# Stick-breaking weights as running sums against differences of neighbouring values, and adaLN's rows moved to other places in the filler

## The chip, the cores and the metric

One Trainium2 chip, one core. The metric is the device time of one execution in microseconds (us); before: median 1586.23 us of 3 runs (1585.62 to 1587.53). A core has a TensorE (PE) for matrix products, whose weight loads are listed apart as PEld, VectorE (DVE), ScalarE (ACT) and GpSimd (POOL) for elementwise work, and SyncE (SP), which here issues all DMAs. Each runs its instructions in program order; they meet by semaphores.

## The reference, cut to what matters

One layer: adaLN modulation, a projection to queries, keys and values, two attention groups side by side, an output projection, a feed-forward layer. 1024 prompt rows, and 64 sample rows with 1024 cached keys; everything in float32. The change touches the second attention group, "stick-breaking", 8 heads of 64:

```python
z = jnp.einsum('bqhd,bkhd->bhqk', qs.astype(f32), ks.astype(f32)) * scale
earlier = k_pos[None, :] < q_pos[:, None]
log_keep = jnp.where(earlier, jax.nn.log_sigmoid(-z), 0.0)
between = lax.cumsum(log_keep, axis=3, reverse=True) - log_keep
w = jnp.where(earlier, jnp.exp(jax.nn.log_sigmoid(z) + between), 0.0)
osb = jnp.einsum('bhqk,bkhd->bqhd', w, vs.astype(f32))
```

With s = sigmoid(z) and k = sigmoid(-z) = 1 - s: the weight of key j is s[j] times the product of k over all later keys that the query may see. The other place is adaLN, `silu(c) @ w_ada + b_ada`: six vectors of 1024 for each of two requests, from a weight of 1024 x 6144.

## The kernel before

The program has three stages: the attention (to some 720 us), the output projection with the second normalisation (to some 840 us), and the feed-forward layer (to the end).

The attention goes through eight units: units 0 to 3 are the four differential heads, units 4 to 7 are pairs of stick-breaking heads. A unit has eight steps for the prompt and one for the samples, put somewhere into the next unit's steps (those of units 3 and 7 stand near the end of their own). A step of class `Stick` is (u, q, hd): 256 queries, that is two blocks t = 2q and 2q+1 of 128, of one head. Its `score` makes, for each t and each chunk of up to 512 keys, two matmuls (L575, L576) into a PSUM bank, on ACT sigmoid(z) and sigmoid(-z) (L738, L739), on POOL the causal mask of the last 128 columns of both (`earlier`, L720), and then `stick`: on DVE a running product over k from the right (a scan, L712), a multiplication of s by it, shifted by one column (L713), and on POOL one column where two chunks meet (L715). `apply` transposes these weights on PE (L586), splits them into a high and a low part on ACT and DVE (L64, L65; the kernel computes float32 products as sums of products of such parts), and multiplies with the values (L759, L760).

The loop over the steps issues `apply` of one step merged with `score` of the next, and between their pieces a filler: the projections of the coming unit, `proj(u, g)` for three groups g of 384, 384 and 320 rows, each needed at a fixed step (`need`: group 0 at the unit's first step, group 1 at its third, group 2 at its seventh). Each piece is given a cost, and the ratio of the costs to the next need sets how much filler goes beside a step. adaLN's remaining twelve pieces of 256 columns (`ada_rows`, 16 matmuls each from two loads of 512 KB, L197 and L201) are filler too: two behind group 2 of units 2 to 5, one behind that of unit 6, three behind that of unit 7, the last with a due time "end". Values come out of `proj_v` transposed: ACT copies them from PSUM (`vf`, L530), `natural` transposes them on PE (L459, bank `pn`) for the output in memory, and the same bank is split into V's two parts.

What the code issues is then put in order for each engine by the compiler's own model of time, so that the order on an engine follows neither the code's order nor the chip's measured times.

Of the kernel before, what the change touches and what calls it, by code (L numbers as in the profile page):

```python
# [10 lines left out]
F32 = mybir.dt.float32  # L11
# [3 lines left out]
ALU = mybir.AluOpType  # L15

P = 128
D = 1024
KT = D // P
TP = 1024  # L20
# [10 lines left out]
def fr(ap):  # L31
    return ap.bitcast(F32)


def build(tc, I, O):
    nc = tc.nc
    ctx = ExitStack()
    sb = ctx.enter_context(tc.tile_pool(name="sb", bufs=1))
# [8 lines left out]
    def big(name, tag, shape, dt=F32R):  # L47
        return sb.tile(shape, dt, tag=tag, name=name, bufs=BUFS[tag])

    def small(shape, name, tag, dt=F32, bufs=2):  # L50
        return sb.tile(shape, dt, tag=tag, name=name, bufs=bufs)

    def brief(shape, name, tag, dt=F32, bufs=2):
        return atp.tile(shape, dt, tag=tag, name=name, bufs=bufs)

    def bank(name, tag):
        return pp.tile([P, 512], F32, tag=tag, name=name)
# [4 lines left out]
    def split(src, hi, lo, eh=None, el=None):  # L62

        (eh or nc.scalar.copy)(hi, src)  # L64
        (el or nc.vector).tensor_tensor(lo, src, fr(hi), ALU.subtract)  # L65

    def halves(name, n=2):
        return [big(f"{name}_{i}", "s", [P, 512], F32) for i in range(n)]


    ident = sb.tile([P, P], F32, name="ident")
# [24 lines left out]
    def x_rows(m):  # L96
        return (x_p[m * P : (m + 1) * P, :], P) if m < 8 else (x_s, TS)
# [200 lines left out]
    def dense_T(ps, w, act, g, ks=range(KT)):  # L298

        n = GRP[g][1]  # L300
        (wh, wl), (hh, hl) = w, act[g]
        for k in ks:
            mm(ps[:, :n], lhsT=wh[:, k, :], rhs=hh[:, k, :n], start=(k == 0), stop=False)  # L303
            mm(ps[:, :n], lhsT=wh[:, k, :], rhs=hl[:, k, :n], start=False, stop=False)  # L304
            mm(ps[:, :n], lhsT=wl[:, k, :], rhs=hh[:, k, :n], start=False, stop=(k == 7))  # L305
            yield 3 * n / 2400
# [133 lines left out]
    def pad_queries(u, m, t):  # L440
        r = slice(64 * m, 64 * m + 64)
        nc.gpsimd.tensor_copy(QZ[m][r], fr(U[u]["Q"][m][r, P * t : P * t + 2 * P]))  # L442

    def family(u):
        return (0, u * P) if u < 4 else (1, (u - 4) * P)
# [6 lines left out]
    def natural(f, u, g, out, name):  # L452

        fam, uc = family(u)
        c0, n = GRP[g]
        nt = 3 if g < 2 else 2
        pt = bank("pn" + name, "pv")
        for i in range(nt):
            nc.tensor.transpose(pt[:, i * P : (i + 1) * P], f[:, i * P : (i + 1) * P], ident)  # L459
        if g == 2:  # L460
            nc.tensor.transpose(pt[:TS, 256:384], f[:, 256:320], ident)
        o = brief([P, 3, P], "o" + name, "vf", bufs=1)
        ptv = pt[:, :384].rearrange("p (t c) -> p t c", t=3)
        nc.vector.tensor_copy(o[:, :nt], ptv[:, :nt])
        load(out[fam][c0 : c0 + nt * P, uc : uc + P].rearrange("(t p) c -> p t c", p=P), o[:, :nt])
        if g == 2:
            nc.vector.tensor_copy(o[:TS, 2], ptv[:TS, 2])
            load(out[2 + fam][:, uc : uc + P], o[:TS, 2])
        return ptv, o

    U = [dict() for _ in range(8)]

    def proj_q(u, g, wq):
        c0, n = GRP[g]
        qs = -0.125 if u < 4 else 0.125
        if g == 0:
            U[u]["Q"] = [big(f"Q{u}{m}", "qk", [P, TP]) for m in range(2)]
        Q = U[u]["Q"]
        if u + g:
            ps = bank(f"pq{u}{g}", "pj")  # L480
            yield from dense_T(ps, wq, hT, g)
        else:
            ps = PS[0]
        w = min(n, TP - c0)
        for m in range(2):
            r, o = slice(64 * m, 64 * m + 64), slice(64 - 64 * m, 128 - 64 * m)
            nc.scalar.mul(Q[m][r, c0 : c0 + w], ps[r, :w], qs)
            nc.vector.scalar_tensor_tensor(Q[m][o, c0 : c0 + w], ps[r, :w], qs, fr(Q[m][r, c0 : c0 + w]), ALU.mult, ALU.subtract)
        if g == 2:
            qsm = brief([P, TS], f"qsm{u}", "ms", bufs=1)  # L490
            nc.scalar.mul(qsm, ps[:, 256:320], qs)
            load(smD[u, :, 0, :], qsm)

    def proj_k(u, g, wk):
        c0, n = GRP[g]
        if g == 0:
            U[u]["Kd"] = [big(f"K{u}{m}", "qk", [P, TP]) for m in range(2)]
            U[u]["Kl"] = big(f"Kl{u}", "qk", [P, TP])
        Kd, Kl = U[u]["Kd"], U[u]["Kl"]
        if u + g:  # L500
# [18 lines left out]
    def proj_v(u, g, wv):  # L519
        c0, n = GRP[g]  # L520
        if g == 0:
            U[u]["V"] = big(f"V{u}", "v", [P, 8, 2, P])
        V = U[u]["V"]
        if u + g:
            ps = bank(f"pv{u}{g}", "pj")
            yield from dense_T(ps, wv, hT, g)
        else:
            ps = PS[2]
        vf = small([P, 384], f"vf{u}{g}", "kf", bufs=2)
        nc.scalar.copy(vf[:, :n], ps[:, :n])  # L530
        ptv, o = natural(vf, u, g, vout, f"v{u}{g}")
        if g == 2:
            load(smV[u], o[:TS, 2])
        ms = slice(3 * g, min(3 * g + 3, 8))
        src = ptv[:, : ms.stop - ms.start]
        if u < 4:
            h_, l_ = V[:, ms, 0, :], V[:, ms, 1, :]
        else:
            q4 = V.rearrange("p m a (b d) -> p m (a b) d", b=2)
            h_, l_ = q4[:, ms, 0::3, :], q4[:, ms, 1:3, :]  # L540
            src = src.rearrange("p t (a d) -> p t a d", a=2)
        split(src, h_, l_)
        yield 0.33
# [35 lines left out]
    def chunks(W):  # L579
        return [(c, min(512, W - c)) for c in range(0, W, 512)]  # L580
# [124 lines left out]
    def stick(s, kp):  # L705


        n = len(s)
        for c in reversed(range(n)):
            w = s[c].shape[-1]  # L710
            k = kp[c][:, (1 if c == 0 else 0) : w][:, ::-1]
            nc.vector.tensor_tensor_scan(k, k, k, 1.0 if c == n - 1 else kp[c + 1][:, 0:1], ALU.mult, ALU.bypass)  # L712
            nc.vector.tensor_tensor(s[c][:, : w - 1], s[c][:, : w - 1], kp[c][:, 1:w], ALU.mult)  # L713
            if c < n - 1:
                nc.gpsimd.tensor_tensor(s[c][:, w - 1 : w], s[c][:, w - 1 : w], kp[c + 1][:, 0:1], ALU.mult)  # L715

    def earlier(s, kp, n):

        for a, f in ((s, 0.0), (kp, 1.0)):
            nc.gpsimd.affine_select(a, a, pattern=[[-1, n]], compare_op=ALU.is_gt, fill=f, base=0, channel_multiplier=1)  # L720

    class Stick:
# [7 lines left out]
        def score(self):  # L730
            u, q, hd = self.u, self.q, self.hd
            self.w = []
            for t in (2 * q, 2 * q + 1):
                ch = chunks(P * (t + 1))
                s, kp = ([a[:, :w] for a, (_, w) in zip(halves(f"{x}{self.name}{t}", len(ch)), ch)] for x in "sk")
                for c, (c0, w) in enumerate(ch):
                    ps = qk(u, hd, t, c0, w, f"pz{self.name}{t}{c}")
                    nc.scalar.activation(s[c], ps, AF.Sigmoid)  # L738
                    nc.scalar.activation(kp[c], ps, AF.Sigmoid, scale=-1.0)  # L739
                    yield 0.43 * w / 512  # L740
                earlier(s[-1][:, -P:], kp[-1][:, -P:], P)
                stick(s, kp)
                self.w.append(s)

        def apply(self):
# [212 lines left out]
    fill = Filler()  # L958
# [10 lines left out]
    steps = [st for sec in sections for st in sec]  # L969
    need = []  # L970
    for u in range(8):
        sec = [st for st in sections[u] if not isinstance(st, Sample)]
        for st, g in zip((sec[0], sec[2], sec[6]), range(3)):
            need.append((steps.index(st), (u, g)))
    need.append((len(steps) + 1, "end"))
    cost = [st.cost for st in steps]
    drain(proj(0, 0))
    ready_1()
# [2 lines left out]
    rows = chain(gate_rows(2 * D, I["g_post_mix"], "r1", 0, ("s", "s")), mod2)  # L981
    rows2 = gate_rows(5 * D, I["g_post_ffn"], "r2", 1, ("s", "s"))

    def some(rows, n):

        for c in rows:
            if c is None:
                n -= 1
                if n == 0:
                    return  # L990
            else:
                yield c

    others = {2: (rows, 2, 2), 3: (rows, 2, 2), 4: (rows, 2, 2), 5: (rows, 2, 2), 6: (rows, 1, 1), 7: (rows, 3, 3)}
    for u in range(8):
        for g in range(3):
            if u + g:
                fill.add(proj(u, g), 12, (u, g))
            if g == (2) and u in others:
                gen, n, c = others[u]  # L1000
                fill.add(some(gen, n), c, "end" if u == 7 else None)
    steps[0].ready()
    drain(steps[0].score())
    prev = None
# [42 lines left out]
    for m in range(NTT):  # L1047
        g, off = m // 3, (m % 3) * P
        hi, lo = mT[g]
        src, rows = x_rows(m)  # L1050
# [219 lines left out]
```

## Time and profile before

| what | value |
|---|---|
| median of 3 runs | 1586.23 us |
| profiled execution, its span | 1589.58 us, 1587.9 us |
| instructions | 23684 |
| busy PE, PEld, DVE, ACT, POOL | 96%, 86%, 62%, 44%, 23% of the span |
| mean granted TensorE clock | 0.973 |

The median and the profiled execution differ by 3.3 us; 1.7 us of the profiled time lie outside its span. The busy shares are means over three stages that differ: the feed-forward layer, over half of the time, has PE full and DVE half idle, the stick-breaking units have DVE nearly full. A share by stage is therefore read, not that of the whole. [...]

### The profile page before, as it was taken

What the parts mean: (1) busy time and instruction counts of PE and PEld (TensorE: products, weight loads), DVE (VectorE), ACT (ScalarE), POOL (GpSimd) and SP (SyncE); (2) the same over time, 40 slices, a digit from 0 to 9 for tenths busy, and PEclk for the clock granted to TensorE, in tenths of its full rate; (3) what the DMA queues carried; (4) which work ended last, traced back from release to release, by engine and by line L of the source; (5) the groups of instructions that cost most, each with busy time, mean ns of one, the idle gap of its engine ahead of it and who ended that gap; (6) DMA issues with size and microseconds to landing.
All of it is one profiled execution on the core that took longest, in us unless ns stands there. A gap on an engine that the chain in (4) does not pass through costs nothing.

```text
span 1587.9 us, 23684 instructions
## 1 busy us (share of the span) xinstructions
PE 1517.0 (96%) x8682; PEld 1357.9 (86%) x8682; DVE 987.2 (62%) x1880; ACT 703.3 (44%) x1665; POOL 366.7 (23%) x580
## 2 busy tenths in 40 slices
PE   6899999999999999789999999999999999999998
PEld 3689988988888889667889888999999899999896
DVE  3777676778789888995552455445544445544447
ACT  3867675766666667656563221121221121221132
POOL 0444352526353434451120000000000000000003
PEclk9999999998999999879999999999999999999999
DMA  9322142432322222364220222021111011111025
GB/s 309 115 60 87 55 116 84 135 95 76 95 74 85 69 70 78 103 208 161 97 63 27 80 80 78 17 79 53 54 42 52 28 41 53 54 41 53 27 80 179
DMA packets 152518, 133.22 MB, mean 84 GB/s; under 512 B 11233, under 2 KB 136274, under 8 KB 152402
## 3 DMA queue, kind: packets, MB, share of 16 engines
q1 hardware_dynamic: 152402, 131.71, 27.2%
q8 instruction: 68, 1.11, 0.3%
q14 instruction: 48, 0.39, 0.1%
HBM read 108.59 MB, written 23.09 MB: 83 GB/s over the span
## 4 chain that ended last, share of the span: by engine, by line
PE 74%; DVE 12%; issue 4%; ACT 3%; DMA 2%; POOL 1%; SPq 0%; POOLq 0%; DVEq 0%; ACTq 0%
PE pu L303 8%; PE pu L304 8%; PE pu L305 8%; PE pd L1145 8%; PE pd L1146 8%; PE pd L1148 7%; DVE k L712 4%; PE py L1059 2%; PE py L1060 2%; PE pt L586 2%; DVE s L713 2%; PE py L1062 2%; PE pq L304 1%; PE pq L303 1%; PE pq L305 1%
## 5 line engine op out<-in xcount | busy, mean ns | idle before, releaser
L1152 DVE TENSOR_TENSOR acc<-pd,acc 128x512 f32<-128x512 f32 x252 | 171.9, 687 | 113.3 <-PE pd L1148 107.2
L1130 ACT ACTIVATE sq<-pu 128x384 f32<-128x384 f32 (+1 forms) x96 | 45.2, 471 | 310.8 <-PE pu L305 310.8
L1131 DVE TENSOR_TENSOR sq<-sq 128x384 f32<-128x384 f32 (+1 forms) x96 | 72.1, 751 | 174.7 <-ACT sq L1130 174.7
L65 DVE TENSOR_TENSOR al<-pt,ah 128x512 fp32r<-128x512 f32 (+2 forms) x128 | 75.5, 599 | 25.7 <-ACT ah L64 24.9
L575 PE MATMUL pz<-K,Q 128*128 128x512 f32 (+2 forms) x192 | 74.8, 393 | 6.4 <-ACT k L739 2.2
L64 ACT CAST ah<-pt 128x512 fp32r<-128x512 f32 (+2 forms) x128 | 65.4, 523 | 33.6 <-PE pt L586 23.2
L586 PE MATMUL pt<-ident,s 128*128 128x128 f32 x432 | 73.7, 288 | 3.3 <-DVE s L713 2.6
L624 ACT ACTIVATE s<-s,mn 128x512 f32<-128x512 f32 (+3 forms) x96 | 58.5, 611 | 26.7 <-DVE mn L660 25.4
L576 PE MATMUL pz<-Kl,qz 128*128 128x512 f32 (+2 forms) x192 | 69.8, 369 | 0.0
L712 DVE TENSOR_TENSOR_SCAN k<-k 128x127 f32<-128x127 f32 (+3 forms) x64 | 62.1, 980 | 4.3 <-POOL k L720 4.0
L713 DVE TENSOR_TENSOR s<-s,k 128x383 f32<-128x383 f32 (+3 forms) x96 | 62.9, 662 | 1.4
L586 PEld LDWEIGHTS pt<-ident,s 128*128 128x128 f32 x432 | 53.1, 147 | 7.6 <-DVE s L713 3.3
L65 DVE TENSOR_TENSOR rl<-sq,rh 128x384 fp32r<-128x384 f32 x64 | 35.7, 558 | 37.9 <-ACT rh L64 37.9
L738 ACT ACTIVATE s<-pz 128x512 f32<-128x512 f32 (+2 forms) x96 | 48.1, 501 | 16.5 <-PE pz L576 12.0
L575 PEld LDWEIGHTS pz<-K,Q 128*128 128x128 f32 x192 | 38.3, 200 | 15.1 <-ACT k L739 4.5
L64 ACT CAST rh<-sq 128x384 fp32r<-128x384 f32 x64 | 32.9, 514 | 40.2 <-DVE sq L1131 38.2
L739 ACT ACTIVATE k<-pz 128x512 f32<-128x512 f32 (+2 forms) x96 | 48.4, 504 | 4.9 <-DVE k L712 4.0
L442 POOL CAST qz<-Q 64x256 fp32r<-64x256 f32 x64 | 34.7, 542 | 66.3 <-PE pz L576 63.9
L760 PE MATMUL po<-al,V 128*128 128x256 f32 (+1 forms) x160 | 43.5, 306 | 6.7 <-DVE al L65 6.6
L759 PE MATMUL po<-ah,V 128*128 128x256 f32 (+1 forms) x160 | 44.9, 292 | 0.5 <-ACT ah L64 0.5
L720 POOL TENSOR_SCALAR_AFFINE_SELECT s<-s 128x128 f32<-128x128 f32 x64 | 30.1, 470 | 63.6 <-ACT s L738 62.9
L660 DVE CUSTOM_DVE_ANT_0 s<-pz,T 128x512 f32<-128x512 f32 (+3 forms) x64 | 37.2, 585 | 10.8 <-PE pz L576 10.3
(1227 smaller groups left out, 5211.3 us busy)
## 6 DMA issues: line engine op xcount, KB each, us to landing
arr<-in_w_ada SPq DMA_DIRECT2D x16, 512.0 KB
arm<-in_w_ada SPq DMA_DIRECT2D x16, 512.0 KB
ar<-in_w_ada SPq DMA_DIRECT2D x10, 512.0 KB
mixD<-mx SPq DMA_DIRECT2D x32, 128.0 KB
xr<-in_x_prompt SPq DMA_DIRECT2D x16, 256.0 KB
xD<-xr SPq DMA_DIRECT2D x16, 256.0 KB
xy<-xD SPq DMA_DIRECT2D x8, 512.0 KB
out_y_prompt<-xy SPq DMA_DIRECT2D x16, 256.0 KB
```

What stands on the lines that cost most here:

```text
L64: (eh or nc.scalar.copy)(hi, src)
L65: (el or nc.vector).tensor_tensor(lo, src, fr(hi), ALU.subtract)
L303: mm(ps[:, :n], lhsT=wh[:, k, :], rhs=hh[:, k, :n], start=(k == 0), stop=False)
L304: mm(ps[:, :n], lhsT=wh[:, k, :], rhs=hl[:, k, :n], start=False, stop=False)
L305: mm(ps[:, :n], lhsT=wl[:, k, :], rhs=hh[:, k, :n], start=False, stop=(k == 7))
L575: mm(ps[:, :w], lhsT=S["Q"][m][:, qt], rhs=S["Kd"][m][:, c0 : c0 + w], start=True, stop=False)
L586: nc.tensor.transpose(pt[:kr, i * P : (i + 1) * P], a, ident)
L712: nc.vector.tensor_tensor_scan(k, k, k, 1.0 if c == n - 1 else kp[c + 1][:, 0:1], ALU.mult, ALU.bypass)
L1145: mm(ps, lhsT=rh[:, off : off + P], rhs=wh[:, cols], start=(j == 0), stop=False)
L1146: mm(ps, lhsT=rh[:, off : off + P], rhs=wl[:, cols], start=False, stop=(m == 8 and end))
L1148: mm(ps, lhsT=rl[:, off : off + P], rhs=wh[:, cols], start=False, stop=end)
L1152: nc.vector.tensor_tensor(acc[m][:, cols], ps, acc[m][:, cols], ALU.add)
```

## The change

`stick` is replaced, for the prompt, by `taken`. Let C[j] be the sum of the weights of key j and all later ones. Then C[j] = s[j] + k[j] C[j+1], which is one scan with multiply and add; and the sum over j of w[j] v[j] equals the sum over j of C[j] (v[j] - v[j-1]), with v[-1] = 0. So the values are replaced by the differences of neighbouring rows, which POOL makes from `vf` for units 4 to 7 (`df`) and PE transposes into a bank of its own (`pdv`); the bank of `natural` then only serves the output. Only s is masked, since a zero in s keeps the sum at zero wherever the query sees nothing. The samples keep the old form. adaLN's pieces stand one behind group 0 and one behind group 1 of units 2 to 7, and have no due time of their own.

```diff
+    vlast = sb.tile([P, 1], F32, name="vlast")
...
         nc.scalar.copy(vf[:, :n], ps[:, :n])
+        w = min(n, TP - c0)
+        if u >= 4:
+            df = small([P, 384], f"df{u}{g}", "kf", bufs=2)
+            if g == 0:
+                nc.gpsimd.tensor_copy(df[:, 0:1], vf[:, 0:1])
+            else:
+                nc.gpsimd.tensor_tensor(df[:, 0:1], vf[:, 0:1], vlast, ALU.subtract)
+            nc.gpsimd.tensor_tensor(df[:, 1:w], vf[:, 1:w], vf[:, 0 : w - 1], ALU.subtract)
+            if g < 2:
+                nc.gpsimd.tensor_copy(vlast, vf[:, w - 1 : w])
         ptv, o = natural(vf, u, g, vout, f"v{u}{g}")
...
+        if u >= 4:
+            yield 0.33
+            pt = bank(f"pdv{u}{g}", "pj")
+            for i in range(ms.stop - ms.start):
+                nc.tensor.transpose(pt[:, i * P : (i + 1) * P], df[:, i * P : (i + 1) * P], ident)
+            ptv = pt[:, :384].rearrange("p (t c) -> p t c", t=3)
...
+    def taken(s, kp):
+        n = len(s)
+        for c in reversed(range(n)):
+            k, d = kp[c][:, ::-1], s[c][:, ::-1]
+            nc.vector.tensor_tensor_scan(d, k, d, 0.0 if c == n - 1 else s[c + 1][:, 0:1], ALU.mult, ALU.add)
...
-                earlier(s[-1][:, -P:], kp[-1][:, -P:], P)
-                stick(s, kp)
+                d = s[-1][:, -P:]
+                nc.gpsimd.affine_select(d, d, pattern=[[-1, P]], compare_op=ALU.is_gt, fill=0.0, base=0, channel_multiplier=1)
+                taken(s, kp)
...
-    need.append((len(steps) + 1, "end"))
...
-    others = {2: (rows, 2, 2), 3: (rows, 2, 2), 4: (rows, 2, 2), 5: (rows, 2, 2), 6: (rows, 1, 1), 7: (rows, 3, 3)}
     for u in range(8):
         for g in range(3):
             if u + g:
                 fill.add(proj(u, g), 12, (u, g))
-            if g == (2) and u in others:
-                gen, n, c = others[u]
-                fill.add(some(gen, n), c, "end" if u == 7 else None)
+            if u > 1 and g < 2:
+                fill.add(some(rows, 1), 1)
```

First place: VectorE in the last unit, scoring its step q = 3 of the first head. Names read unit, underscore, q, head, t, and then the chunk: s7_306_1 is chunk 1 of block 6. Before:

```order
L712 SCALAR_TENSOR_TENSOR k7_306_1_8809<-k7_306_1_8809 128x384
L65 TENSOR_TENSOR al7_202_8752<-pt7_202_8747,ah7_202_8751 128x384
L713 TENSOR_TENSOR s7_306_1_8807<-s7_306_1_8807,k7_306_1_8809 128x383
L712 SCALAR_TENSOR_TENSOR k7_306_0_8808<-k7_306_0_8808,k7_306_1_8809 128x511
L65 TENSOR_TENSOR al7_210_8803<-pt7_210_8797,ah7_210_8802 128x512
L713 TENSOR_TENSOR s7_306_0_8806<-s7_306_0_8806,k7_306_0_8808 128x511
```

And the same scans now:

```order
L743 SCALAR_TENSOR_TENSOR s7_306_1_8632<-k7_306_1_8634,s7_306_1_8632 128x384
L65 TENSOR_TENSOR al7_202_8597<-pt7_202_8592,ah7_202_8596 128x384
L743 SCALAR_TENSOR_TENSOR s7_306_0_8631<-k7_306_0_8633,s7_306_1_8632,s7_306_0_8631 128x512
L65 TENSOR_TENSOR Vn7_8752<-vn7_8714,Vn7_8752 64x128
L743 SCALAR_TENSOR_TENSOR s7_307_1_8662<-k7_307_1_8664,s7_307_1_8662 128x512
```

The multiplications L713 are gone between the scans; a scan reads k and s, and goes on from the chunk behind it.

Second place: TensorE where one of adaLN's pieces stands (`ar`, `arm`: the loaded weights; `poS`, `pt`: the samples' products and the transposes of a step). Before, behind group 2 of unit 4:

```order
L586 MATMUL pt5_010_6229<-ident_66,s5_010_0_6107 128x128
L586 MATMUL pt5_010_6229<-ident_66,s5_011_0_6140 128x128 x2
L201 MATMUL pam210_6454<-arm2100_6455,sc_106 32x256 x4
L201 MATMUL pam210_6454<-arm2101_6483,sc_106 32x256 x4
L575 MATMUL pz5_2041_6429<-K50_5569,Q50_5448 128x128
```

Now, behind group 1 of unit 4:

```order
L620 MATMUL poS3_4946<-cv30_4842,ahS30_4952 128x256
L459 MATMUL pnv41_5026<-ident_66,vf41_5020 128x128 x3
L551 MATMUL pdv41_5033<-ident_66,df41_5022 128x128 x3
L201 MATMUL pam201_5039<-arm2010_5040,sc_106 32x256 x4
L201 MATMUL pam201_5039<-arm2011_5048,sc_106 32x256 x4
L621 MATMUL poS3_4946<-cv30_4842,alS30_4953 128x128
```

The new transposes of `df` stand right behind those of `vf` in TensorE's queue, and adaLN's piece behind them.

Third place: GpSimd, where the new operations stand among the masks. Before, in unit 7's second q:

```order
L720 AFFINE_SELECT s7_102_0_8399<-s7_102_0_8399 128x128
L715 TENSOR_TENSOR ss6_1_8306<-ss6_1_8306,skt6_8310 128x1
L720 AFFINE_SELECT k7_102_0_8400<-k7_102_0_8400 128x128
L715 TENSOR_TENSOR ss6_0_8305<-ss6_0_8305,sk6_1_8309 128x1
L442 CAST qz0_493<-Q70_7604 64x256
```

Now, in unit 6's last q, with the first group of unit 7's values:

```order
L770 AFFINE_SELECT s6_307_1_7688<-s6_307_1_7688 128x128
L537 COPY df70_7801<-vf70_7799 128x1
L540 TENSOR_TENSOR df70_7801<-vf70_7799 128x383
L542 COPY vlast_499<-vf70_7799 128x1
L770 AFFINE_SELECT s6_316_1_7768<-s6_316_1_7768 128x128
```

Each block has one mask instead of two, and three operations per group of values stand among them.

## Rows read from the trace of the kernel before

**Rows 1.** The page: busy time by engine; tenths in 40 slices; granted clock.
```profile
PE 1517.0 (96%) x8682; PEld 1357.9 (86%) x8682; DVE 987.2 (62%) x1880; ACT 703.3 (44%) x1665; POOL 366.7 (23%) x580
PE   6899999999999999789999999999999999999998
DVE  3777676778789888995552455445544445544447
PEclk9999999998999999879999999999999999999999
```
**Rows 2.** Busy time by stretch; first line: the columns.
```profile
core 0: us, PE busy (x) PEld busy (x) DVE busy (x) ACT busy (x) POOL busy (x), PEclk, DMA share, GB/s
380.00:400.00 20.00, 16.26 (x88) 13.54 (x87) 17.13 (x25) 11.52 (x29) 13.73 (x19) 0.74 0.21 66
400.00:460.00 60.00, 59.24 (x412) 56.00 (x405) 48.16 (x87) 38.80 (x93) 18.96 (x38) 1.00 0.30 90
460.00:490.00 30.00, 24.86 (x169) 21.39 (x168) 29.05 (x45) 19.51 (x48) 18.61 (x25) 0.89 0.49 142
490.00:520.00 30.00, 30.00 (x201) 29.45 (x200) 27.72 (x47) 18.66 (x43) 8.23 (x18) 1.00 0.09 28
520.00:570.00 50.00, 44.09 (x279) 40.81 (x278) 44.78 (x70) 30.54 (x74) 24.12 (x39) 0.90 0.33 97
570.00:630.00 60.00, 59.66 (x407) 58.20 (x406) 51.89 (x89) 42.30 (x102) 18.91 (x45) 1.00 0.20 54
630.00:720.00 90.00, 74.19 (x402) 59.39 (x401) 84.74 (x132) 55.89 (x123) 44.23 (x48) 0.83 0.49 154
```
**Rows 3.** The same view for line L713 alone, DVE busy.
```profile
380.00:400.00 20.00, 7.06 (x8) 0.74 0.21 66
460.00:490.00 30.00, 7.41 (x10) 0.89 0.49 142
520.00:570.00 50.00, 10.00 (x16) 0.90 0.33 97
630.00:720.00 90.00, 19.42 (x24) 0.83 0.49 154
```
**Rows 4.** Groups by line, VectorE: scans and multiplications; busy us, mean ns, idle before.
```profile
L712 DVE TENSOR_TENSOR_SCAN k<-k 128x127 f32<-128x127 f32 (+3 forms) x64 | 62.1, 980 | 4.3 <-POOL k L720 4.0
L712 DVE TENSOR_TENSOR_SCAN k<-k,k 128x511 f32<-128x511 f32 x32 | 42.3, 1322 | 0.0
L713 DVE TENSOR_TENSOR s<-s,k 128x383 f32<-128x383 f32 (+3 forms) x96 | 62.9, 662 | 1.4
L713 DVE TENSOR_TENSOR ss<-ss,sk 128x511 f32<-128x511 f32 x8 | 5.5, 691 | 0.0
L713 DVE TENSOR_TENSOR sst<-sst,skt 128x63 f32<-128x63 f32 x4 | 2.9, 718 | 0.1
```
**Rows 5.** Line L712's samples: duration ns min/median/max, first and last start.
```profile
L712 DVE TENSOR_TENSOR_SCAN skt<-skt x4: 292/292/294, 456.9 to 674.1; 128x64 f32<-128x64 f32 x4
L712 DVE TENSOR_TENSOR_SCAN sk<-sk,skt x4: 1271/1278/1312, 457.4 to 676.5; 128x512 f32<-128x512 f32 x4
```
**Rows 6.** Groups by line, GpSimd.
```profile
L720 POOL TENSOR_SCALAR_AFFINE_SELECT k<-k 128x128 f32<-128x128 f32 x64 | 27.4, 428 | 7.0 <-ACT k L739 5.7
L715 POOL TENSOR_TENSOR s<-s,k 128x1 f32<-128x1 f32 x32 | 15.3, 478 | 40.8 <-DVE k L712 38.1 <-PE pz L576 2.7
L65 POOL TENSOR_TENSOR h1l<-xt,h1h 128x384 fp32r<-128x384 f32 x8 | 8.3, 1052 | 3.2 <-ACT h1h L64 3.1
```
**Rows 7.** Timeline of one group's values: start, length, engine, line.
```profile
452.43 0.49 ACT L530 COPY vf<-pv 128x384 f32<-128x384 f32 x1
458.77 0.52 PE L459 MATMUL pnv<-ident,vf 128*128 128x128 f32 x3
```
**Rows 8.** Busy time by stretch, in the differential heads (unit 2).
```profile
200.00:240.00 40.00, 36.40 (x238) 33.50 (x237) 29.21 (x79) 28.07 (x81) 20.93 (x30) 0.91 0.45 130
240.00:280.00 40.00, 39.49 (x241) 33.16 (x241) 26.91 (x81) 22.44 (x69) 10.52 (x23) 0.92 0.24 70
```

## The prediction, made before the changed kernel was run

> **What bounds the kernel now.** The page comes first [rows 1]: PE is busy 96% of the span and DVE 62%, which alone would say that work taken off DVE is worth nothing. The slices say where that mean comes from. From the nineteenth slice on (some 720 us, the output projection and the feed-forward layer) PE reads 9 and DVE 4 or 5; nothing of the change lies there, and I leave that time as it is. Slices 10 to 18 are the stick-breaking units: DVE reads 8 and 9, PE falls to 7 and 8, and the granted clock has dips.
>
> The second view is the busy time by stretch of that stage [rows 2]. It falls into two kinds of stretch, which take turns. In three of them (400 to 460, 490 to 520, 570 to 630; 150 us) PE is busy 148.9 us at full clock: PE bounds them. In the other four (380 to 400, 460 to 490, 520 to 570, 630 to 720; 190 us) DVE is busy 17.13 + 29.05 + 44.78 + 84.74 = 175.7 us, or 92.5%, while PE is busy 159.4 us at clocks from 0.74 to 0.90. Those are the long steps of each unit (q = 2 and 3) and all of the end: DVE bounds them, and PE waits for it and drops to its lower clock in places. What DVE is spared counts in these four stretches and nowhere else.
>
> The third view is DVE's groups by line [rows 4]: in the stick-breaking steps the scans (L712) take 62.1 + 42.3 = 104.4 us and the multiplications behind them (L713) 62.9 us.
>
> **The multiplications that go.** All 96 of the prompt, 62.9 us of DVE. In the four DVE-bound stretches line L713 takes 7.06 + 7.41 + 10.00 + 19.42 = 43.9 us [rows 3]. That includes the samples', which stay: 5.5 + 2.9 = 8.4 us [rows 4], and I count all of them as lying there. So 35.5 us leave DVE where it bounds: 140.2 us are left. At the same 92.5% the stretches would take 151.6 us, which is 38.4 us less.
>
> What is late next is PE. Its 159.4 us at the clocks it had are 16.26 x 0.74 + 24.86 x 0.89 + 44.09 x 0.90 + 74.19 x 0.83 = 135.4 us at full clock. So in 151.6 us it would be nearly 90% busy even at full clock, and at its present clocks it would not fit: with 159.4 us of work and the 1% of idle time that it has in the PE-bound stretches, the four take 161 us, 29 us less than now. Between 29 and 38 I take 31, nearer to the PE end, because two engines near 90% seldom hand over without gaps. The upper end of what could come is PE at full clock, 135.4 / 0.99 = 137 us, and DVE without a gap, 140.2 us: some 50 us less. The lower end is nothing, if PE's waits in these stretches stay where they are.
>
> **The scan that takes their place.** The same number of scans over the same columns (one more at chunk 0), now with two different inputs and an add. The trace shows no scan with an add. Its nearest row is the scan with a bypass: 64 columns take 292 ns and 512 take 1278 [rows 5], so (1278 - 292) / 448 = 2.2 ns for a column. The scans of the four units cover 128 x (1 + ... + 8) = 4608 columns for each of 8 heads, 36,864 in all. From below: the add is free, 0. From above: the loop through two operations takes twice as long per column, 36,864 x 2.2 ns = 81 us more of DVE. I take 0, the row for the same instruction.
> [...] No run here shows a scan with an add.
>
> **Masks and single columns on POOL.** One mask of two goes, 27.4 us, and the 32 single-column products, 15.3 us [rows 6]. New are, for 12 groups of values, one subtraction over 383 or 255 columns (at most 1052 ns, the row of 128x384) and 20 operations on one column at 478 ns: 12.6 + 9.6 = 22.2 us at most. POOL ends up with about 20 us less. It bounds nothing (18.6 of 30 us in its fullest stretch but one, [rows 2]), so I count 0; that the scan waits for one mask less is 4.0 us of DVE idle time at most [rows 4], which I leave within the 31.
>
> **The new transposes and the longer way to V.** 3 + 3 + 2 transposes in each of four units, 32 in all. Three of the same shape take 0.52 us in the timeline [rows 7], 0.17 each: 5.5 us of PE. In the DVE-bound stretches they fill gaps; in the PE-bound ones they are on the path, and some two thirds of the groups lie there: +3.5 us. They must wait for POOL: 2 x 0.48 + 1.05, about 2.0 us after ACT's copy, plus what stands ahead in POOL's queue. In the trace PE comes to the transposes of the same copy 458.77 - 452.92 = 5.85 us after the copy is done, and that is the shortest distance of the 11 groups from 360 to 720 us [rows 7]. So PE's own backlog covers the 2 us. Were the cover gone, PE would stand for up to 2 us in each of 12 groups, 24 us, with the scores and products of the steps behind it.
>
> **adaLN's pieces.** Their instructions, 16 matmuls and two loads for each of 12, stay the same in number; each queue is passed by the same work in another place. Before, two stand together behind a unit's last group, in the DVE-bound steps; now one by one beside other projections. In unit 2, where two stand, the granted clock is 0.91 and 0.92 [rows 8]: (1 - 0.91) x 36.4 + (1 - 0.92) x 39.5 = 6.4 us of clock lost, and 4.1 us of PE idle. From this view alone I can't say that the pieces do this. Bounds: -10.5 us if they do all of it and it goes, +10.5 us if the loads now collide elsewhere to the same extent. I take -3.
>
> **The sum.** -31 + 3.5 - 3 = -30.5 us. The profiled execution, 1589.6 us, becomes 1559; the median of the runs, 3.4 us lower, 1586.2 - 30.5 = 1556.
>
> **The rivals.**
> - *PE reaches full clock in the four stretches.* Then the relief is up to 50 us rather than 31. For it: the clock falls just where DVE is late. Against it: DVE's 140.2 us would then have no gap at all, and they have 14 us of gaps now. Half of the way, 41 us: 1546, down to 1536 at the end of it.
> [...]
> [...]
> - *PE waits for the differences.* The 24 us above, if PE's backlog shrinks with DVE's relief or POOL's queue holds `df` up: 1556 + 24 = 1580.
> - *The change does not do what it says to the time.* PE in the four stretches follows an order fixed ahead, and its waits move from L713 to the sigmoids or the copies: within 3 us of 1586.
> - *Slower: the add doubles the scan.* +81 us of DVE against -62.9 is 18 us more; 62% of it (the share of L713 that lies in the DVE-bound stretches, 43.9 of 62.9 + 8.4 us) is 11 us, and with 3.5 us of transposes the time is some 1600. It decides from 1.7 ns more per column (62.9 us over 36,864 columns), that is a scan of 512 columns at 2.15 us where it now takes 1.28.
>
> **How the numbers follow.** Forecast 0.52 (1546 to 1567 around 1556), full clock 0.13, slow end 0.15, waits for the differences 0.07, no change 0.05, slower 0.08. A measurement of this kernel can tell about 0.2%, 3 us, from no change. Faster by more than that: 0.52 + 0.13 + 0.15 + 0.07 = 0.87; within it 0.05; slower 0.08. The range reaches from 1536, near the lower end of the full-clock case, to 1582, past the waits for the differences; outside lie the slower case, half of the no-change case, and some 0.05 below.
>
> **What would show it.** Right: DVE's multiplications in the prompt's steps gone and its scans of 512 columns at 1.25 to 1.35 us; the stick-breaking stage, 370 to 720 us, about 30 us shorter, nearly all of it in the stretches of q = 2 and 3; PE busier there and its clock nearer 1; the feed-forward stage of the same length. Wrong: a scan near 2 us; PE idle before the transposes of `pdv`, released by POOL; a clock near 0.67 over the whole end; DVE still at 92% in those stretches, or the four stretches shorter and the three others longer by as much.

## The result and the profile after

Device time of the runs, median: 1585.92 us before (4 runs, 1585.37 to 1587.53) and 1566.78 us after (4 runs, 1563.63 to 1568.11). The ratio is 0.9871, with a 95% interval from 0.9858 to 0.9885: 19.1 us faster, where 30 were forecast. The profiled execution took 1567.92 us, with a span of 1566.2.

The page of the changed kernel, the lines that answer to [rows 1]:
```profile
PE 1504.5 (96%) x8714; PEld 1343.9 (86%) x8714; DVE 917.5 (59%) x1784; ACT 704.6 (45%) x1665; POOL 331.0 (21%) x516
PE   5899999999999999879999999999999999999998
DVE  3776768676768576875453454444554544544447
PEclk9999999999999999989999999999999999999999
```
DVE lost 96 instructions and 69.7 us and reads 5 to 8 in slices 10 to 18, where it read 7 to 9; PE gained 32 matmuls (the transposes), and its slices 17 and 18 still read below 9. The slices are means over 39 us. To see what the stage itself gained, cut it at the same events in both kernels: a unit ends where its last store of mixed rows (`mixD<-mx`) starts. Busy time by unit (4, 5, 6, 7; columns as in [rows 2]) of the kernel before:
```profile
383.83:456.15 72.32, 68.07 (x441) 62.73 (x442) 58.62 (x100) 45.48 (x109) 25.47 (x45) 0.93 0.28 82
456.15:543.13 86.98, 79.91 (x541) 75.05 (x540) 79.14 (x125) 55.56 (x132) 38.23 (x66) 0.96 0.27 77
543.13:624.03 80.90, 76.58 (x497) 72.77 (x497) 72.21 (x119) 52.92 (x125) 30.89 (x57) 0.94 0.24 70
624.03:721.29 97.26, 80.16 (x442) 65.27 (x441) 91.12 (x144) 60.99 (x136) 48.56 (x58) 0.84 0.50 153
```
The same view of the changed kernel:
```profile
372.19:440.57 68.38, 67.18 (x454) 62.99 (x454) 49.07 (x82) 49.09 (x113) 21.82 (x33) 1.00 0.24 70
440.57:520.48 79.91, 77.30 (x525) 70.97 (x524) 58.80 (x97) 54.92 (x128) 28.46 (x43) 0.98 0.31 90
520.48:607.59 87.11, 80.51 (x530) 74.79 (x529) 60.47 (x98) 52.92 (x126) 25.08 (x44) 0.94 0.21 65
607.59:702.08 94.49, 78.32 (x460) 65.48 (x458) 71.43 (x124) 64.98 (x146) 38.13 (x45) 0.91 0.48 149
```
Three things are to be read here. DVE was spared 61.3 us of the stage (301.1 to 239.8), close to the 62.9 us of the multiplications. The stage itself became only 7.6 us shorter (337.5 to 329.9). Another 11.6 us stand ahead of it, since its first mark moved from 383.83 to 372.19, and 2.5 us behind it; that makes the 21.7 us by which the two spans differ. And in unit 7 no engine is full any more: of 94.5 us PE is busy 78.3 and DVE 71.4. PE's idle time there was 17.1 us and is 16.2.

How far such marks can be trusted: a variant that differs from the changed kernel only in where adaLN's last three pieces stand (e8 below) has the same work ahead of the first mark, reaches it at 381.1, and ends the stage at 701.8, level with 702.08. So a share between "ahead of the stage" and "in the stage" is good to some 9 us. I argue from whole times below, and what is read between such marks there is a hint of where time went, not a measurement.

What PE itself waited for in that stage (line waited for: us in total, times, longest), before:
```profile
PE po L760 <- DVE al L65: 6.6, 7, 2.0
PE poS L603 <- DVE alS L65: 4.0, 3, 1.9
PE ptS L586 <- DVE ss L713: 2.8, 1, 2.8
PE pt L586 <- DVE s L713: 2.6, 2, 2.4
```
And after:
```profile
PE po L789 <- DVE al L65: 14.1, 9, 7.3
PE pcm L209 <- DVE Rm L224: 3.1, 2, 2.6
PE pnv L459 <- DVE mx L808: 2.2, 1, 2.2
```
The prompt's waits for a multiplication (L713) are gone, as they must be. In their place the product with V (`po`) waits longer for the low part of the weights (`al`), once for 7.25 us. That one wait has its cause in the timeline (start, length, engine, line) of the changed kernel:
```profile
666.96 2.99 POOL L65 TENSOR_TENSOR wo5l<-wo5r,wo5h 128x1024 fp32r<-128x1024 f32 x1
667.73 2.76 DVE L731 TENSOR_TENSOR ss<-ss,sk 128x511 f32<-128x511 f32 x1
669.91 2.78 POOL L65 TENSOR_TENSOR wo6l<-wo6r,wo6h 128x1024 fp32r<-128x1024 f32 x1
670.42 3.35 DVE L730 TENSOR_TENSOR_SCAN sk<-sk,sk 128x511 f32<-128x511 f32 x1
673.70 0.53 DVE L65 TENSOR_TENSOR al<-pt,ah 128x384 fp32r<-128x384 f32 x1
674.28 0.58 PE L789 MATMUL po<-al,V 128*128 128x256 f32 x1 [7.25 <-DVE al L65]
675.34 0.66 DVE L731 TENSOR_TENSOR ss<-ss,sk 128x511 f32<-128x511 f32 x1
```
The same multiplication of 511 columns takes 0.66 us alone and 2.76 beside GpSimd's low part of the output weights. It starts 0.77 us after GpSimd's operation and ends 0.54 us behind it; the scan after it ends 1.08 us behind the next one. Both look nearly as if they had begun when GpSimd was done; that the one waits for the other is my reading of these times, and no run shows it by itself.

Last, the new instructions. The scan with an add (source view: ns min/median/max, first to last start), and the differences and their transposes:
```profile
L743 DVE TENSOR_TENSOR_SCAN s<-k,s,s x32: 1258/1276/3273, 388.0 to 680.7; 128x512 f32<-128x512 f32 x32
```
```profile
L540 POOL TENSOR_TENSOR df<-vf x12: 602/818/825, 339.3 to 639.2; 128x383 f32<-128x383 f32 x8, 128x255 f32<-128x255 f32 x4
```
```profile
L551 PE MATMUL pdv<-ident,df x32: 270/273/422, 340.8 to 641.1; 128*128 128x128 f32 x32
  POOL df L540: 0.3, 1
```
1276 ns against 1278 with a bypass [rows 5]: the add costs nothing. The last line says that PE stood before these transposes once, for 0.3 us, for GpSimd. The distance that was to cover them shrank all the same: in the changed kernel one copy of `vf` ends at 523.91 and PE comes to its transposes (`pnv`) at 524.16, 0.25 us later, where 5.85 was the least before.

### The profile page after: what moved, and what is told of

It is laid out like the page before. It is cut to its first block, busy times and chain, and to the rows that moved or that the text cites. A ratio compares the mean times of both kernels' runs of the same rounds, so it can differ in the third digit from the quotient of the medians.

```text
span 1566.2 us, 23554 instructions
## 1 busy us (share of the span) xinstructions
PE 1504.5 (96%) x8714; PEld 1343.9 (86%) x8714; DVE 917.5 (59%) x1784; ACT 704.6 (45%) x1665; POOL 331.0 (21%) x516
## 4 chain that ended last, share of the span: by engine, by line
PE 84%; DVE 5%; ACT 3%; issue 3%; POOL 1%; DMA 1%; DVEq 0%; POOLq 0%; ACTq 0%
PE pu L303 8%; PE pu L305 8%; PE pu L304 8%; PE pd L1171 8%; PE pd L1172 8%; PE pd L1174 7%; PE pt L604 2%; PE py L1085 2%; PE py L1086 2%; PE pq L303 2%; PE pq L304 2%; PE pq L305 2%; PE py L1088 2%; PE pk L304 2%; PE pk L303 2%
## 5 line engine op out<-in xcount | busy, mean ns | idle before, releaser
L604 PE MATMUL pt<-ident,s 128*128 128x128 f32 x432 | 70.5, 278 | 0.6 <-issue 0.4
L743 DVE TENSOR_TENSOR_SCAN s<-k,s 128x128 f32<-128x128 f32 (+1 forms) x64 | 53.8, 849 | 13.3 <-ACT k L767 7.3
L442 POOL CAST qz<-Q 64x256 fp32r<-64x256 f32 x64 | 29.9, 468 | 105.1 <-PE pz L594 93.6
L789 PEld LDWEIGHTS po<-al,V 128*128 128x128 f32 x160 | 31.2, 195 | 18.8 <-DVE al L65 18.0
L743 DVE TENSOR_TENSOR_SCAN s<-k,s,s 128x512 f32<-128x512 f32 x32 | 43.3, 1353 | 0.4
L64 ACT CAST r<-sq 128x320 fp32r<-128x320 f32 x32 | 14.8, 461 | 62.9 <-DVE sq L1157 62.9
```

Source lines behind the costliest of these rows:

```text
L604: nc.tensor.transpose(pt[:kr, i * P : (i + 1) * P], a, ident)
L743: nc.vector.tensor_tensor_scan(d, k, d, 0.0 if c == n - 1 else s[c + 1][:, 0:1], ALU.mult, ALU.add)
```

## The experiments

Each kernel was timed beside the kernel before on the same chip. Differences are of medians to the kernel before as timed there; an interval of the ratio is some 2 to 4 us to either side, so a difference between two rows is good to some 3 to 5 us.

| kernel | edit | median us (n) | difference | ratio, 95% |
|---|---|---|---|---|
| changed | both parts | 1566.78 (4) | -19.1 | 0.9871 [0.9858, 0.9885] |
| e1 | before, pieces moved | 1591.96 (6) | +6.4 | 1.0047 [1.0030, 1.0065] |
| e2 | changed, pieces in their old places | 1579.82 (12) | -5.7 | 0.9960 [0.9943, 0.9977] |
| e5 | changed + unread multiplications | 1596.81 (6) | +10.3 | 1.0080 [1.0061, 1.0099] |
| e9 | e2 + unread multiplications | 1598.51 (6) | +13.2 | 1.0082 [1.0063, 1.0102] |
| e3 | before, pieces moved in pairs | 1589.86 (8) | +4.3 | 1.0033 [1.0018, 1.0049] |
| e6 | before, all but the last three moved | 1595.29 (6) | +8.7 | 1.0070 [1.0052, 1.0088] |
| e11 | changed, pieces' matmuls twice | 1570.61 (6) | -14.7 | 0.9911 [0.9893, 0.9928] |
| e12 | before, pieces' matmuls twice | 1596.13 (6) | +10.8 | 1.0067 [1.0051, 1.0084] |
| e7 | e1, wo's low parts on DVE | 1587.17 (12) | +0.6 | 1.0013 [0.9998, 1.0028] |
| e4 | changed, wo's low parts on DVE | 1567.30 (5) | -18.3 | 0.9895 [0.9877, 0.9913] |
| e8 | changed, last three pieces at the end | 1562.49 (6) | -24.1 | 0.9866 [0.9842, 0.9890] |
| e10 | e8 + e4 | 1559.61 (5) | -25.7 | 0.9831 [0.9809, 0.9853] |

**The two halves: e1 and e2.** e1 is the kernel before with adaLN's pieces moved and nothing else:
```diff
...
-            if g == (2) and u in others:
-                gen, n, c = others[u]
-                fill.add(some(gen, n), c, "end" if u == 7 else None)
+            if u > 1 and g < 2:
+                fill.add(some(rows, 1), 1)
```


> The kernel before with only adaLN's pieces moved. Theory A (the pieces carry most of the gain): by the changed kernel's trace 17 us less of idle and low-clock PE time from 160 to 400 us, where only the pieces differ, so some 1571 us (1566 to 1576), with the granted clock at 1.00 from 160 to 370 us. Theory B (the spared multiplications carry it, as the prediction's sum had it): 3 us, so 1583 us.

e2 is the changed kernel with this edit undone (the sums alone).

> The changed kernel with adaLN's pieces back in their old places and their due time. Theory A: 4 to 6 us below the kernel before, 1580 to 1582 us, with the clock dips from 200 to 280 us as before. Theory B: 1569 us or less, nearly the changed kernel's 1567.

Measured: e1 is 6.4 us *slower*, which no theory had, and e2 5.7 us faster, as theory A had it. The halves add up to +0.7 and together they make -19.1: each half does much better with the other one there. Now look at 160 to 320 us, around the stretch from which I had priced the pieces, first before, then in e1:
```profile
160.00:320.00 160.00, 154.35 (x1000) 139.41 (x999) 113.18 (x328) 104.31 (x307) 65.64 (x104) 0.96 0.33 97
```
```profile
160.00:320.00 160.00, 159.18 (x1059) 144.21 (x1058) 114.34 (x343) 106.96 (x313) 65.11 (x105) 1.00 0.36 106
```
Clock 0.96 to 1.00, PE's idle time 5.7 to 0.8 us, 59 matmuls more. That PE idles less goes with the move: in the four kernels with the pieces in their old places (before, e2, e9, e12) it idles 5.5 to 6.8 us there, in all the others 0.6 to 3.4. In the old places part of it is a wait for the pieces' weights, 2.3 to 3.8 us. The first line is e2's stretch; the others are this wait from 160 us to the first mark, before (384 us) and in the changed kernel (372 us):
```profile
160.00:320.00 160.00, 153.25 (x1029) 138.54 (x1027) 115.75 (x336) 107.16 (x317) 67.61 (x107) 0.99 0.35 104
PE par L201 <- DMA arr<-in_w_ada: 3.7, 5, 1.6
PE par L201 <- DMA arr<-in_w_ada: 0.6, 1, 0.6
```
The clock does not go with it: e2 has 0.99 with the pieces in their old places. So the 0.96 before says little about them. e1 is slower all the same, so the loss lies behind this stretch. By unit, e1:
```profile
380.87:449.32 68.45, 66.36 (x422) 60.00 (x423) 55.69 (x99) 42.96 (x102) 23.00 (x41) 0.92 0.27 78
449.32:534.61 85.29, 79.71 (x529) 72.00 (x528) 71.22 (x124) 56.10 (x132) 38.69 (x66) 0.98 0.29 85
534.61:621.68 87.07, 79.11 (x504) 70.62 (x504) 74.97 (x123) 52.20 (x124) 35.27 (x56) 0.96 0.21 60
621.68:724.75 103.07, 80.73 (x430) 67.71 (x428) 84.73 (x138) 62.29 (x139) 56.33 (x58) 0.85 0.42 128
```
Units 6 and 7 are 6.2 and 5.8 us longer than before, against 3.9 and 1.7 us gained in units 4 and 5. In unit 7, PE is busy as long as before (80.7 against 80.2) and idle 22.3 us instead of 17.1.

**DVE's relief alone: e5 and e9.** Behind each of the prompt's scans a multiplication that nobody reads gives DVE its old load back, in the changed kernel (e5) and in e2 (e9):
```diff
             nc.vector.tensor_tensor_scan(d, k, d, 0.0 if c == n - 1 else s[c + 1][:, 0:1], ALU.mult, ALU.add)
+            w = s[c].shape[-1]
+            nc.vector.tensor_tensor(kp[c][:, : w - 1], s[c][:, : w - 1], kp[c][:, 1:w], ALU.mult)
```


> The changed kernel with a multiplication of the old size put back behind every prompt scan, its result read by nothing, so VectorE's load is the old one and the chain from scan to transposes stays the new one. Theory L (with adaLN's pieces moved, VectorE's load decides): the gain is lost and the time comes to that of the pieces alone, 1585 to 1595 us. Theory R (what helps is the shorter chain from scan to transposes, one mask and the single columns that POOL no longer does): within 8 us of the changed kernel, 1575 us at most.

> The running sums with adaLN's pieces in their old places, and the unread multiplication behind every prompt scan, so VectorE's old load. Against the same kernel without it (1580 us) this prices VectorE's relief where the pieces are not moved. Theory I (with the pieces in the old places the relief is worth much less than the 30 us that it is worth with them moved): 1586 to 1594 us. Rival (the relief is worth 30 us in both, and the old places cost the sums something else): 1605 to 1613 us.

Measured: +10.3 and +13.2 us against the kernel before. So taking the multiplications off DVE is worth 29.4 us where the pieces are moved (e5 to changed) and 18.9 where they are not (e9 to e2). e5 lies 2 us above theory L's range, e9 between its two theories. In e5 the added multiplications take 61.1 us, near the 62.9 that went [rows 4]. They are not the old ones in every respect: the weights can go on to their transposes before them. By unit, e5:
```profile
372.70:449.90 77.20, 70.44 (x459) 65.40 (x458) 65.20 (x103) 50.38 (x115) 24.83 (x33) 0.96 0.24 74
449.90:537.35 87.45, 79.62 (x527) 73.08 (x527) 74.59 (x122) 53.95 (x127) 32.19 (x43) 0.96 0.26 76
537.35:628.44 91.09, 81.36 (x536) 75.30 (x535) 74.13 (x124) 54.91 (x130) 28.51 (x46) 0.94 0.21 65
628.44:731.52 103.08, 79.67 (x448) 67.50 (x446) 85.52 (x140) 63.27 (x142) 38.12 (x44) 0.87 0.43 132
```
Up to its first mark e5 keeps pace with the changed kernel (372.70 and 372.19), and then it loses 8.8, 7.5, 4.0 and 8.6 us, in each unit some. Of these 28.9 us PE was idle 21.1 and busy longer 7.8. This is the cleanest pair here: the gain of the relief is real and, by these marks, spread over the whole stage.

**Why do the moved pieces lose? e3 and e6.** e3 sets two pieces together behind group 0 of units 2 to 7 instead of one each behind two groups; e6 leaves the last three at the end:
```diff
-            if u > 1 and g < 2:
-                fill.add(some(rows, 1), 1)
+            if u > 1 and g == 0:
+                fill.add(some(rows, 2), 2)
```
```diff
...
+            if g < 2 and (1 < u < 6 or (u, g) == (6, 0)):
+                fill.add(some(rows, 1), 1)
+            if (u, g) == (7, 2):
+                fill.add(some(rows, 3), 3, "end")
```


> The kernel before with adaLN's pieces two by two behind group 0 of units 2 to 7, so moved but still in pairs. Theory A1 (what counts is that they leave the place behind a unit's last group): within 4 us of the kernel that has them singly behind groups 0 and 1. Theory A2 (what counts is that they come singly): no better than half of that kernel's gain, 1578 us or more, with clock dips now beside group 0.

> The kernel before with nine of adaLN's pieces moved to single places behind groups 0 and 1 of units 2 to 6, the last three left behind group 2 of unit 7 with their due time. Theory E (moving the pieces gains some 8 us up to the end of unit 5 and loses some 11 in the last two units, where VectorE bounds and the filler is missing): 1577 to 1582 us. Rival (the loss of the moved pieces is not tied to the last three): 1588 us or more, as with all moved.

Measured: +4.3 and +8.7 us, both with intervals that overlap e1's. So neither singles in place of pairs nor the lack of filler at the end is shown to be the cause.

**Are the pieces free in their old places? e11 and e12.** Each piece's matmuls run a second time, into the unused half of its bank, 192 matmuls in all, in the changed kernel (e11) and in the kernel before (e12). In both, adaLN's gate and second modulation then differ from the reference's.
```diff
...
+            for i in range(4 if ps2 is not None else 0):
+                mm(ps2[32 * i : 32 * i + 32, 256:], lhsT=sc[:, 4 * q + i, :], rhs=raw[:, i, :], start=(q == 0), stop=(q == 1), skip_group_check=True)
```


> The changed kernel with every matmul of adaLN's twelve pieces in the attention done twice, the second into an unused half of its bank. Eight of these matmuls take 0.57 us in the trace of the kernel before, so the twelve pieces gain about 14 us of PE work. Theory P (the pieces now stand where PE is the bound, so their work is on the path): 10 to 16 us more, 1577 to 1583. Rival (PE has room there): under 5 us more, 1572 or less.

> The kernel before with the same matmuls done twice, 14 us of PE work more in the old places. Theory P (eight of the twelve pieces stand where PE waits for VectorE, and cost next to nothing there): 0 to 6 us more than before, 1586 to 1592. Rival (they are on the path in the old places as well): 10 us or more, 1596 or more.

Measured: 4.4 us more than the changed kernel, and 10.8 more than the kernel before. The added matmuls alone (0 to 800 us, line L208, PE and PEld busy), in e11 and in e12:
```profile
0.00:800.00 800.00, 19.75 (x192) 6.81 (x192) 0.99 0.36 111
0.00:800.00 800.00, 18.56 (x192) 7.34 (x192) 0.96 0.35 108
```
On the page PE's busy time grows by less, 7.3 us (1504.5 to 1511.8) and 5.3 us (1517.0 to 1522.3), since other work takes less of it in these traces. The result went the wrong way round for the theory that pieces are free where DVE is the fuller engine and cost their time where PE is. In the old places, 18.6 us more of matmuls cost 10.8 us of time, and 8 of the 12 pieces stand in the stick-breaking units there, most of them beside a DVE that is busy 92.5% [rows 2]; in the new places 19.8 us cost 4.4. So those stretches are not DVE's alone. I take it that PE's work stands in the same loop of scores, sigmoids, scans, transposes and products; no run shows the loop by itself. (`pam210`, shown above as a piece behind group 2 of unit 4 before the change, is one of unit 5's; it runs at 474.6 us.)

**The output weights' low parts: e7 and e4.** They go from GpSimd to DVE, which takes away GpSimd's operations of 2.3 to 3.4 us beside DVE's in the end, in e1 (e7) and in the changed kernel (e4):
```diff
-        wo.append(weights(w_out[:, k, :], [P, 1024], f"wo{k}", ("w", "w") if k < 3 else ("qk", "qk"), el=nc.gpsimd))
+        wo.append(weights(w_out[:, k, :], [P, 1024], f"wo{k}", ("w", "w") if k < 3 else ("qk", "qk"), el=nc.vector))
```


> The kernel before with all of adaLN's pieces moved, and the low parts of the output projection's weights on VectorE instead of GpSimd. Theory C (the loss of the last unit comes from GpSimd's splits of these weights, which stand earlier now and slow VectorE's operations): 1584 us or less, against 1592 with them on GpSimd. Rival (VectorE's own load decides there; the splits add 11 us to it): 1592 to 1602 us.

> The changed kernel with the low parts of the eight output-projection weights on VectorE instead of GpSimd. Theory C (GpSimd's two-input operations of 2.4 to 3.0 us slow VectorE's down at the end: a multiplication of 2.76 us for 0.67, a scan of 3.35 for 1.28, and PE waits 7.25 us behind them): that wait falls below 2 us and the time by 4 to 8 us, to some 1560. Rival: the 8 operations of about 1.35 us are 11 us more on VectorE, which is 84% busy there, and the time stays or rises, 1567 to 1575 us.

Measured: e7, between its two theories, is 0.6 us above the kernel before, so this edit takes 5 to 6 us off e1, though not surely all of its loss: with its interval, up to 4.4 us may be left. That the collision is what the moved pieces cost is not shown by this. The kernel before has it too, with the pieces in their old places:
```profile
679.61 3.31 POOL L65 TENSOR_TENSOR wo1l<-wo1r,wo1h 128x1024 fp32r<-128x1024 f32 x1 [0.65 <-ACT wo1h L64]
680.68 3.06 DVE L712 TENSOR_TENSOR_SCAN k<-k 128x384 f32<-128x384 f32 x1
688.40 2.36 POOL L65 TENSOR_TENSOR wo3l<-wo3r,wo3h 128x1024 fp32r<-128x1024 f32 x1
688.79 2.51 DVE L713 TENSOR_TENSOR s<-s,k 128x511 f32<-128x511 f32 x1
```
Elsewhere in this trace the same scan takes 0.95 us and the multiplication 0.69. The kernel before with these low parts on DVE was not run; it might gain as much. e4's longest wait for `al` is 2.5 us instead of 7.3:
```profile
PE po L789 <- DVE al L65: 6.3, 8, 2.5
```
and yet its time is that of the changed kernel (1567.3). A wait of 7.25 us taken out of the middle of the end gave nothing there.

**A better version: e8 and e10.** e8 is the changed kernel with its last three pieces due at the end, as they were; e10 has e4's edit too.

> The changed kernel with the last three of adaLN's pieces left at the end, behind group 2 of unit 7 with their due time, the other nine singly behind groups 0 and 1 of units 2 to 6. Theory E (with VectorE relieved the end no longer needs them): within 4 us of the changed kernel, 1563 to 1571. Rival (filler at the end keeps the clock up): 1555 to 1562 us. Other rival (they cost at the end what they cost before): 1572 us or more.

> The changed kernel with two of the edits together: the last three pieces at the end, and the output projection's low parts on VectorE. If both small gains are real and add up: 1556 to 1560 us. If they are scatter: 1563 to 1569 us, as the changed kernel.

Measured: e8's ratio can't be told from the changed kernel's. e10 is 25.7 us faster than the kernel before, and its interval (to 0.9853) ends just below the changed kernel's (from 0.9858): it beats that one too. The end, 640 to 700 us, in the changed kernel and in e10:
```profile
640.00:700.00 60.00, 45.99 (x254) 36.80 (x253) 50.16 (x85) 42.99 (x94) 23.96 (x21) 0.91 0.49 156
```
```profile
640.00:700.00 60.00, 50.91 (x285) 41.10 (x284) 51.13 (x91) 42.16 (x85) 7.30 (x12) 0.91 0.63 214
```
PE is busy 4.9 us longer at the same clock. e10's stage ends at 694.8, and up to there the difference is the same (45.8 against 40.8 us). 1.7 us of it are adaLN's pieces; that the rest is what the collision no longer spoils is likely but not shown. Neither edit showed a gain that could be told apart by itself.

## Why the prediction was right in its sign and wrong by 11 us

The terms against the runs, by two orders of the same three steps:

| term | forecast | pieces first | sums first |
|---|---|---|---|
| multiplications gone | -31 | -29.4 (e5 to changed) | -18.9 (e9 to e2) |
| add, GpSimd, transposes, longer way to V | +3.5 | +3.9 (e1 to e5) | +13.2 (before to e9) |
| adaLN's pieces | -3 | +6.4 (before to e1) | -13.4 (e2 to changed) |
| sum | -30.5 | -19.1 | -19.1 |

**Right.** The scan's add: 0, at 1276 ns for 512 columns against 1278 with a bypass; the rival on the slower side, at 2150, did not come. GpSimd: its differences over many columns take 602 to 825 ns, below the 1052 that I allowed, and it bounds nothing. PE hardly waits for the differences (0.3 us, where 24 were the rival's price), though not for the reason given: the backlog of 5.85 us went down to 0.25 in one place. DVE's relief, where it comes last, measured 29.4 us, against 31. That they come so near is in part luck: the 31 were to come from four stretches alone, e5 loses time in every unit, and by the other order the relief is worth 18.9.

**The step that failed** is the third term and the way it entered the sum. I took -3 for the pieces, with bounds of 10.5 to either side, from the clock and the idle time of unit 2 alone [rows 8]. PE's idle time did go there, but the clock that I counted as lost is 0.98 from 200 to 280 us in e2, with the pieces in their old places; and their new places in units 6 and 7 were not priced at all. With DVE's load as it was, the move costs 6.4 us: 9.4 of the 11.4 that are missing, by this order of steps. By the other order it gains 13.4 and the relief is worth only 18.9. So there is no one price for the move: +6.4 in the kernel before, -2.9 with the sums at DVE's old load (e9 to e5, within the scatter), -13.4 with DVE relieved. A sum of terms, each priced with the other parts left as they were, can't give that.

**Behind it stands a reading of [rows 2] that did not hold.** I took four stretches for DVE's, with PE's work free there, and forecast that PE would then be 1% idle. (Of the slices in [rows 1], DVE's read 7 to 9 and not 8 and 9, and PE's fall to 7 and 8 in the last two of nine only.) e12 showed PE's work on the path in the old places; and after the change the stage has 26.6 us of PE idle time left (329.9 less 303.3) while DVE is busy 73% of it. Sparing DVE its 61 us gave back 19 to 29 us of time. That the engines take turns in a loop, and that this is the part that lay in it, is my reading and fits these numbers.

**The rivals.** The slow end, with 0.15 among the chances, came half true: unit 7 is 2.8 us shorter where DVE was spared 19.7, and its clock is 0.91 after 0.84, not back at full. No row and no run shows the clock near 0.67 over the end that was to tell this case. e8 does not show that the missing filler alone did it. Full clock was reached in unit 4 only (1.00, then 0.98, 0.94, 0.91). That nearly all of the gain would lie in the long steps is not borne out: 11.6 of the traces' 21.7 us stand ahead of the stage's first mark, though that mark is only good to some 9 us.

**Open.** Why the pieces' new places cost time beside a loaded DVE and gain beside a relieved one. Taking the low parts away from GpSimd is worth 5 to 6 us in e1 (e7), but the kernel before has these collisions too. Pairs, the last three pieces and free PE work were tried and did not explain it. All instructions of a variant are ordered anew when it is built, e8's mark shows that this alone moves things by 9 us inside the kernel, and how much of each difference it makes was not measured.

## What to carry to other kernels

Where two engines are both 80 to 95% busy in a stage, don't take either for free: here work taken off one came back in part (61 us for 19 to 29), and the end of the sum was not "the next engine at 99%". Filler work that is moved must be priced where it arrives as well as where it leaves, and together with the other edits; run the halves before believing a sum. Look for long two-input operations on GpSimd beside VectorE's (here of 2.3 to 3.4 us, with a multiplication beside them at 2.76 us instead of 0.66), and try another place or engine for them; but measure it, since that was worth 5 to 6 us in e1 and nothing by itself in the changed kernel.

## What was not expected of the hardware

- Two VectorE operations whose inputs all lie in SBUF took 2.6 and 4.2 times as long beside GpSimd's two-input operations: in the timeline above a scan 3.35 us, where 1.28 is its time otherwise [rows 5], and a multiplication 2.76 instead of 0.66. `al`, with one of its inputs in PSUM, took 0.69 us beside such operations (at 642.47 and 662.73 us of the changed kernel).
- A better clock in one stretch was no gain in the whole here. With the pieces' matmuls doubled (e12), the stretch from 160 to 320 us has clock 1.00 where the kernel before has 0.96, 82 matmuls more in as much busy time (56 of them are doubled ones), and the kernel is 10.8 us slower. That the doubled matmuls raise the clock is not shown: e2 has 0.99 there without them. e12's stretch:
```profile
160.00:320.00 160.00, 153.80 (x1082) 139.93 (x1084) 115.22 (x334) 106.68 (x316) 67.54 (x106) 1.00 0.35 102
```
